# Three more projection jobs ahead of the retention heads, their results kept in DRAM

## The chip, the cores and the metric

One NeuronCore of a Trainium2 chip. The metric is device time in microseconds (us) of one execution. Engines by their short names: PE (TensorE, matmuls), DVE (VectorE), ACT (ScalarE), POOL (GpSimd), SP (SyncE, which issues most loads). A change of about 0.2% is what a measurement of this kernel can tell from none.

## What is computed

One inference step of a two-layer decoder for 512 prompt tokens and 8 x 4 sample tokens (544 columns in all), model width 1024: layer 0 mixes with a short gated convolution, layer 1 with multi-scale retention (4 heads, keys of 256, values of 512), each followed by a SwiGLU block (hidden width 2816). Weights are shared by both groups. The part around the change is the retention mixer:

```python
z = x @ w_in                                  # q, k (1024 each), v, g (2048 each)
q, k, v, g = jnp.split(z, [1024, 2048, 4096], axis=-1)
q = rotary(q, pos); k = rotary(k, pos) * (256 ** -0.5)
# per head, chunks of 128 tokens:
scores = jnp.einsum('bhid,bhjd->bhij', qc, kc) * decay
inner  = jnp.einsum('bhij,bhjv->bhiv', scores, vc)
cross  = jnp.einsum('bhid,bhdv->bhiv', qc, S) * cross_w
S_new  = S * chunk_decay + jnp.einsum('bhjd,bhjv->bhdv', kc * state_w, vc)
# group norm over each head's 512 values, gain, then
out = (silu(g) * of) @ w_out
```

All values are fp32. The sample tokens also update a recurrent state per head that is read and written.

## The kernel before

Activations lie transposed: 8 tiles of 128 rows by 544 columns, handled as two halves of 272. Every fp32 matrix is split into a high part and a low part (`split`: ACT copies the rounded high part, DVE subtracts to get the low one), and a product takes three matmuls (high-high, high-low, low-high). A plain projection of one output tile of 128 (`project`, L167 to L182, matmuls at L175) takes 8 k-tiles x 3 x 2 halves = 48 matmuls of 272 columns. Weights are loaded on SP's queue in pieces of 512 KB into three buffers (`wts`), split, and used.

A **Job** (L461) makes two output tiles at once from seven products of half size in the manner of Strassen and Winograd (`weights7` builds the sums of weights; matmuls at L480): 7 x 4 x 3 = 84 matmuls in place of 96. Its weights come in two loads, L434 (`w3`) and then L435 (`w1`); two accumulating DMAs on POOL's queue make low parts. `summed` gathers the products: ACT takes snapshots (L540), DVE adds (L543). The feed-forward layers run as such jobs.

At the end of the first feed-forward layer `ahead` (L785) runs while the sums of the activations for jobs can still be kept: it projects q and k of head 0 plainly, then runs five jobs: two gate tiles of head 0, and the four gate tiles of heads 1 and 2 each (`AHEAD = (1, 2)`). Their results go to DRAM (`qk_made`, `gate_made`) from ACT's queue and are loaded again in the heads.

Then come the four heads in a loop (L1298). In each: `value` (L987) projects the values into four PSUM banks and, after its second weight piece, splits q and k, makes the sample scores and transposes the keys; then state, scores, outputs (`inner`), sample outputs and state updates; each output row is normalized on DVE with a power on POOL (`normalized`), transposed on PE (L1172) and multiplied into the gate on DVE (`gated`). Work that depends on none of that fills in between, through `fill(n)` (n = 0 to 3) and by calls at the head's end:

- head 0: gate tiles 2 and 3 of its own, k of head 1; at the end q of head 1
- heads 1 and 2: the output projection of the previous head (`held_project`, two tiles of 24 matmuls in each fill, from the old gated tiles that `held_parts` splits); at the end k, then q, of the next head
- head 3: its four gate tiles (`gate_project`) in the fills; then the old output projection, tiles 4, 5, 2, 3 at places where normalizations run, the halves of tiles 0 and 1 that come from the old head, and `last_project` with its own.

`qk_project` multiplies the projection with a table that holds decay and the inverse norm (`gt`, L915, scaled by `qk_scale` at L942) and `rotate` turns it (L969 to L974, six DVE operations). Head 0's q and k come from DRAM (`qk_loaded`, L926 and L930).

The order of instructions on each engine is set by a list scheduler at build time: program order is the priority, an instruction takes its turn when the scheduler's model has its inputs ready, and each engine then runs its list strictly in order. `tc.issue_after(ins)` puts an instruction behind another one of the same engine. A tile with `bufs=1` and one tag is one place: its next use waits until the last reader of the previous one is done. `rot1` and `gt` in the pool `kp` are such places; the old halves of `held_parts` use both.

Of the kernel before, what the change touches and what calls it, by code (L numbers as in the profile page):

```python
# [49 lines left out]
def hybrid_decode_kernel(ctx: ExitStack, tc: tile.TileContext, a: dict, o: dict):  # L50
# [76 lines left out]
    rN = resid.tile([P, 6], F32, tag="rN", name="rN")  # L127


    last_load = [None]  # L130

    def parts2(n, pool=None, tags=("wh", "wl")):
        return [(pool or wts).tile([P, n], F32R, tag=t, name=nm(t)) for t in tags]
# [294 lines left out]
    def weights7(src1, src2, sw, adding=False):  # L428

        n = KP * P  # L430
        w3, w1 = [wts.tile([P, 2 * n], F32, tag="w", name=nm("w")) for _ in range(2)]
        w2 = sw.tile([P, 2 * n], F32, tag="w2", name=nm("w2"))
        w4 = sw.tile([P, n], F32, tag="w4", name=nm("w4"))
        last_load[0] = nc.sync.dma_start(w3, src2)  # L434
        last_load[0] = nc.sync.dma_start(w1, src1)  # L435
        a11, a12, a21, a22 = w1[:, :n], w1[:, n:], w3[:, :n], w3[:, n:]
        s2, s1 = w2[:, :n], w2[:, n:]
        nc.vector.tensor_add(s1, a21, a22)
        nc.vector.tensor_sub(s2, s1, a11)
        nc.vector.tensor_sub(a21, a11, a21)  # L440
        nc.vector.tensor_sub(w4, a12, s2)
        p1 = parts2(2 * n)
        (split_adding if adding else mixed)(*p1, w1, src1)
        p2 = parts2(2 * n, sw, ("h2", "l2"))
        split(*p2, w2)
        p3 = parts2(2 * n)
        mixed(*p3, w3, src2)
        p4 = parts2(n, sw, ("h4", "l4"))
        split(*p4, w4)

        def part(p, at):
# [328 lines left out]

    dram = ctx.enter_context(tc.tile_pool(name="dram", bufs=1, space=bass.MemoryType.DRAM))
    qk_made = [dram.tile([P, 2, T], F32, tag=f"qk{w}", name=nm("qkm")) for w in range(2)]
    gate_made = {h: dram.tile([P, 4, T], F32, tag=f"g{h}", name=nm("gm")) for h in (0, *AHEAD)}

    def ahead(tp, fp, sw, operand_tiles):  # L785


        wide("m")
# [44 lines left out]
        def gates(h, n):  # L833
            made = {}

            def tile2():
                if not made:
                    made[0] = tp.tile([P, 2, T], F32, tag="gu", name=nm("gate"))
                return made[0]

            def gate(what, src):
                g = tile2()
                if what == "c21":
                    nc.scalar.activation(g[:, 1, :HT], src, AF.Copy)
                elif what == "c12":
                    r = R.rearrange("p a b -> p (a b)").unsqueeze(1).to_broadcast([P, 2, T])
                    nc.vector.tensor_mul(g, g, r)
                    nc.scalar.activation(g, g, AF.Silu)
                    for i in range(2):
                        nc.scalar.activation(g[:, i, :], g[:, i, :], AF.Copy, scale=g_ret(h * 4 + n + i))  # L850
                    nc.scalar.dma_start(gate_made[h][:, n : n + 2, :], g)

            return Job([a["rtg"][h, n + i] for i in range(2)], operand, sw, summed(tile2, gate))

        jobs = [gates(0, 0)] + [gates(h, n) for h in AHEAD for n in (0, 2)]
        jobs[0].prepare()
        run(jobs, (2, 5, 6), lambda i: None, iter(()))

# [3 lines left out]
    with ExitStack() as c2:  # L862
# [47 lines left out]
        def qk_start(h):  # L910

            st = {}
            gt = kp.tile([P, 2, T], F32, tag="gt", name=nm("gt"), bufs=1)
            with tc.issue_after(last_load[0].ins) if h == 0 else ExitStack():
                nc.sync.dma_start(gt, a["gtab"][h])  # L915
            st["gt"] = gt
            st["rot"] = [
                pool.tile([P, 2, T], F32, tag=f"rot{w}", name=nm("rot"), bufs=1) for w, pool in enumerate((tp, kp))
            ]
            return st  # L920

        def qk_loaded(st):

            for t, src in ((st["rot"][1], qk_made[1]), (st["rot"][0], qk_made[0])):
                with tc.issue_after(last_load[0].ins):
                    nc.sync.dma_start(t, src)  # L926
            for which in (1, 0):
                qk_scale(st, which)
# [11 lines left out]
        def qk_scale(st, which):  # L940
            gi = halves(st["gt"][:, which, :])
            nc.vector.tensor_mul(gi, gi, R)  # L942

        def qk_project(h, st, which, dt, inside=None):

# [154 lines left out]
            return st["gate"][n // 2][:, n % 2, :] if len(st["gate"]) > 1 else st["gate"][0][:, n, :]  # L1100

        def gate_project(h, st, n):
            st.setdefault("gate", [])
            if h == NH - 1 and n % 2 == 0:

                pool, tag = ((kp, "gt"), (qp, "qkhl1"))[n // 2]
                t = pool.tile([P, 2, T], F32, tag=tag, name=nm("gate"), bufs=1)
                st["gate"].append(t)
            elif not st["gate"]:
                st["gate"].append(swapped(True, [P, 4, T], F32, "gate"))  # L1110
# [101 lines left out]
        def sample_outputs(h, st, i):  # L1212
# [7 lines left out]
            with tc.issue_after(last_product[0].ins):  # L1220
                for g in range(4):
# [2 lines left out]
                        start=False, stop=(i == 3), skip_group_check=True,  # L1224
                    )

        def states_update(h, st, i):


# [10 lines left out]
                    )  # L1240
            for w, pu in enumerate(pus):
                Si = S[:, 2 * w : 2 * w + 2, :]
                nc.vector.scalar_tensor_tensor(Si, Si, _gamma(h) ** 4, pu, op0=ALU.mult, op1=ALU.add)  # L1243
            nc.sync.dma_start(rets_out[r, h, dt], S)

        def gated_parts(st):
# [51 lines left out]
        for h in range(NH):  # L1298
            more = h + 1 < NH

            def fill(n):

                if h in AHEAD:
                    for i in range(2):
                        held_project(h, (0, 4, 2, 6)[n] + i)
                elif h:
                    gate_project(h, st, n)
                elif n < 2:

                    gate_project(h, st, n + 2)  # L1310
                else:
                    qk_project(h + 1, nxt, 1, n - 2)

            value(h, st)
            st["S"] = {}
# [19 lines left out]
            if h in AHEAD:  # L1335
                st["gate"] = [swapped(h == 2, [P, 4, T], F32, "gate")]
                nc.sync.dma_start(st["gate"][0], gate_made[h])
            if not more:
                held_parts(h, older)
            yn0 = normalized(inner(h, st, 0))  # L1340
            sample_outputs(h, st, 1)
            yn1 = normalized(inner(h, st, 1))
# [6 lines left out]
                    qk_scale(nxt, which)  # L1349
            with tc.issue_after(last_product[0].ins):  # L1350
                if more:
                    qk_project(h + 1, nxt, int(h > 0), 0)
                else:
                    held_project(h, 4)
            with tc.issue_after(last_product[0].ins):
# [9 lines left out]
                gated(h, st, yn2, 2)  # L1365

            if more:
                qk_project(h + 1, nxt, int(h > 0), 1, inside)
            else:
                held_project(h, 5, single=True)  # L1370
                inside()
                held_project(h, 2, single=True)
            yn3 = normalized(p3)
            if not more:
                held_project(h, 3)
            gated_pair(h, st, (yns, 4), (yn3, 3))
            if more and h:
                qk_project(h + 1, nxt, 0, 0)
                qk_project(h + 1, nxt, 0, 1)
            if not more:  # L1380
                held_project(h, 0, False, single=True)
                held_project(h, 1, False)
# [119 lines left out]
```

## Time and profile before

| what | value |
|---|---|
| median of 3 runs | 1458.8 us (1458.06 to 1460.22) |
| the profiled execution: time, span | 1461.27 us, 1459.5 us |
| mean granted clock of PE | 0.996 |
| busy: PE, DVE, ACT, POOL | 99%, 68%, 45%, 10% of the span |
| DMA | 201.89 MB, mean 138 GB/s |
| jobs ahead | about 598 to 657 us |
| the four heads | about 653 to 1077 us |

All times within the profile are counted from the start of the span. A line of a timeline has start and length in us, engine, source line, operation, the tiles written and read, and in brackets how long the engine was idle before and what released it. SPq and the like are the queue's issues of DMAs. A line number can be a helper's: L190 and L191 are the two halves of every `split`, L175 every plain projection.

### The profile page before, as it was taken

Reading aid. Unit: us, or ns where it says so; the run is one execution under the profiler, and the core shown is the slowest. Engines: PE = TensorE matmul, PEld = TensorE weight load, DVE = VectorE, ACT = ScalarE, POOL = GpSimd, SP = SyncE. Lnnn points to the kernel's source line nnn. Section 1 sums busy time; section 2 is a strip of 40 time slices with the busy share of each in tenths; the row PEclk is TensorE's granted clock in tenths of the full one; section 3 lists DMA queues with packets and bytes.
Section 4 is the critical chain, followed back from the end, with each engine's and each line's share of the span. In section 5 each row is a group of like instructions: output and inputs, shape, how many; then the busy total and the mean of one; then the engine's idle time right before and its main releaser. Section 6 shows DMA issues by size and latency. Waiting matters only on the chain.

```text
span 1459.5 us, 26302 instructions
## 1 busy us (share of the span) xinstructions
PE 1443.8 (99%) x10860; PEld 1369.0 (94%) x10860; DVE 985.7 (68%) x1536; ACT 664.0 (45%) x971; POOL 147.9 (10%) x184
## 2 busy tenths in 40 slices
PE   9999999999999999999999999999999999999997
PEld 8999999999999999997878888878999999999997
DVE  5644679847748648677575765845699848749554
ACT  5222466626526437664223032134386626537334
POOL 0100011101101003210010000000111101101002
PEclk9999999999999999999999999999999999999998
DMA  6222246636536434767353734724666635546432
GB/s 219 82 88 92 86 114 140 150 116 126 143 106 139 124 80 133 195 167 262 125 191 116 258 106 144 274 92 143 175 138 149 153 108 131 131 109 148 119 81 77
DMA packets 84297, 201.89 MB, mean 138 GB/s; under 512 B 8129, under 2 KB 25409, under 8 KB 83921
## 3 DMA queue, kind: packets, MB, share of 16 engines
q1 hardware_dynamic: 67296, 165.91, 35.9%
q0 software_dynamic: 15008, 29.18, 12.2%
q10 hardware_dynamic: 1872, 5.12, 0.9%
q8 instruction: 85, 1.39, 0.4%
q14 instruction: 36, 0.29, 0.1%
HBM read 175.11 MB, written 25.08 MB: 137 GB/s over the span
## 4 chain that ended last, share of the span: by engine, by line
PE 89%; DVE 5%; DMA 3%; ACT 1%; issue 1%; POOL 0%; SPq 0%; DVEq 0%; ACTq 0%; POOLq 0%
PE sm L480 35%; PE mm L175 33%; PE sm L175 7%; PE sm L999 2%; PE sm L1000 2%; PE sm L1001 2%; PE sm L163 2%; PE sm L164 1%; PE sm L165 1%; PE sm L1222 1%; DMA w<-in_ffgu_dram 1%; DVE wl L191 1%; DMA w<-in_rtg_dram 1%; DVE S L1243 1%; DVE ol L191 1%
## 5 line engine op out<-in xcount | busy, mean ns | idle before, releaser
L190 ACT ACTIVATE wh<-w 128x1024 fp32r<-128x1024 f32 (+4 forms) x126 | 115.8, 923 | 318.8 <-PE mm L175 204.9
L480 PE MATMUL sm<-oh,wh 128*128 128x272 f32 x744 | 215.5, 290 | 0.1
L480 PE MATMUL sm<-ol,wh 128*128 128x272 f32 x744 | 214.3, 288 | 0.7 <-DVE ol L191 0.7
L480 PE MATMUL sm<-oh,wl 128*128 128x272 f32 x744 | 213.9, 287 | 0.0
L175 PE MATMUL mm<-xh,wh 128*128 128x272 f32 x844 | 176.3, 290 | 1.1 <-ACT wh L190 1.0
L175 PE MATMUL mm<-xh,wl 128*128 128x272 f32 x844 | 174.5, 289 | 0.4 <-DMA wl<-in_rtqk_dram 0.4
L175 PE MATMUL mm<-xl,wh 128*128 128x272 f32 x844 | 173.9, 287 | 0.0
L480 PE MATMUL sm<-oh,h 128*128 128x272 f32 x568 | 164.1, 289 | 0.5 <-DVE gate L543 0.4
L480 PE MATMUL sm<-oh,l 128*128 128x272 f32 x568 | 163.5, 288 | 0.0
L480 PE MATMUL sm<-ol,h 128*128 128x272 f32 x568 | 163.5, 288 | 0.0
L273 DVE TENSOR_TENSOR x<-x,mm 128x544 f32<-128x544 f32 x90 | 64.7, 719 | 144.7 <-PE mm L175 144.7
L191 DVE TENSOR_TENSOR wl<-w,wh 128x1024 fp32r<-128x1024 f32 (+4 forms) x126 | 134.2, 1071 | 23.7 <-ACT wh L190 22.3
L480 PEld LDWEIGHTS sm<-oh,wh 128*128 128x128 f32 x744 | 139.8, 188 | 2.1 <-ACT gate L540 0.9
L423 ACT ACTIVATE wh<-w 128x1024 fp32r<-128x1024 f32 x97 | 102.8, 1060 | 83.2 <-PE sm L480 56.1
L480 PEld LDWEIGHTS sm<-ol,wh 128*128 128x128 f32 x744 | 139.8, 188 | 0.9 <-DVE ol L191 0.9
L480 PEld LDWEIGHTS sm<-oh,wl 128*128 128x128 f32 x744 | 140.3, 189 | 0.0
L426 POOL DMA_DIRECT2D wl<-in_ffgu_dram x87 | 75.6, 869 | 635.2 <-ACT wl L425 261.5
L175 PEld LDWEIGHTS mm<-xh,wh 128*128 128x128 f32 x844 | 132.2, 188 | 5.4 <-ACT wh L190 1.4
L175 PEld LDWEIGHTS mm<-xh,wl 128*128 128x128 f32 x844 | 131.6, 188 | 0.9 <-DMA wl<-in_rtqk_dram 0.6
L175 PEld LDWEIGHTS mm<-xl,wh 128*128 128x128 f32 x844 | 132.1, 188 | 0.1
L191 DVE TENSOR_TENSOR l<-w,h 128x1024 fp32r<-128x1024 f32 x98 | 93.4, 955 | 27.0 <-ACT h L190 26.4
L480 PEld LDWEIGHTS sm<-oh,h 128*128 128x128 f32 x568 | 107.2, 189 | 1.0 <-ACT wh L423 0.6
(296 smaller groups left out, 3211.8 us busy)
## 6 DMA issues: line engine op xcount, KB each, us to landing
w<-in_ffgu_dram SPq DMA_DIRECT2D x88, 512.0 KB, 3.9
wl<-in_ffgu_dram POOLq DMA_DIRECT2D x87, 256.0 KB, 4.8
w<-in_ffdn_dram SPq DMA_DIRECT2D x96, 192.0 KB, 2.5
S<-in_rets_dram SPq DMA_DIRECT2D x16, 1024.0 KB, 7.0
out_rets_dram<-S SPq DMA_DIRECT2D x16, 1024.0 KB, 4.8
w<-in_cvin_dram SPq DMA_DIRECT2D x21, 512.0 KB, 3.4
w<-in_rtqk_dram SPq DMA_DIRECT2D x16, 512.0 KB, 3.6
w<-in_rtg_dram SPq DMA_DIRECT2D x16, 512.0 KB, 4.1
```

The source lines that it names most:

```text
L163: nc.tensor.matmul(out, lh, rh, start=start, stop=False, skip_group_check=True)
L164: nc.tensor.matmul(out, lh, rl, start=False, stop=False, skip_group_check=True)
L175: last_product[0] = nc.tensor.matmul(half(pt, hf)[:, :HT], w[:, c], act[k][:, hf * HT : (hf + 1) * HT], start=(first and k == ks[0] and i ...
L190: h = nc.scalar.activation(dh, src, AF.Copy)
L191: last_low[0] = nc.vector.tensor_sub(dl, src, dh.bitcast(F32))
L273: last_residual[0] = nc.vector.tensor_add(xk, xk, p)
L423: nc.scalar.activation(wh, w, AF.Copy)
L426: nc.gpsimd.dma_start(wl[:, n:], src[:, n:], accum_op=ALU.add)
L480: last = nc.tensor.matmul(out, w[:, c], b, start=(first and k == 0 and i == 0), stop=(k == KP - 1 and i == 2), skip_group_check=True,)
L999: nc.tensor.matmul(out, xh[kt][:, ts_], wh[:, cw], start=(kt == 0), stop=False)
L1000: nc.tensor.matmul(out, xh[kt][:, ts_], wl[:, cw], start=False, stop=False)
L1001: last = nc.tensor.matmul(out, xl[kt][:, ts_], wh[:, cw], start=False, stop=(kt == KT - 1))
```

## The change

- `ahead` runs eight jobs: the five of before, and three new ones in the order shown below: k of head 2, k of head 3 and the first two gate tiles of head 3. A k job stores its sums unscaled to `k_made` in DRAM.
- In heads 1 and 2, k of the next head is loaded from `k_made`, multiplied by the table and rotated (`k_loaded`); q takes the two places at the head's end that k had, and the two projections after the last `gated_pair` are gone.
- In head 3 the fills are gate tiles 2 and 3, then `held_parts` with old output tiles 2 and 3, then nothing; tiles 2 and 3 leave the end of the head. Gate tiles 0 and 1 are loaded from DRAM.
- The loads of head 0's table and k are ordered behind the load L434 of the last job's weights and no longer behind L435; q's load stays behind L435.

```diff
+    last_load, second_load = [None], [None]
...
-        last_load[0] = nc.sync.dma_start(w3, src2)
+        second_load[0] = nc.sync.dma_start(w3, src2)
         last_load[0] = nc.sync.dma_start(w1, src1)
...
+    k_made = {h: dram.tile([P, 2, T], F32, tag=f"k{h}", name=nm("km")) for h in range(2, NH)}
+    gate_made = {h: dram.tile([P, 4, T], F32, tag=f"g{h}", name=nm("gm")) for h in range(NH)}
...
+            def k(what, src):
+                g = tile2()
+                if what == "c21":
+                    nc.scalar.activation(g[:, 1, :HT], src, AF.Copy)
+                elif what == "c12":
+                    nc.scalar.dma_start(k_made[h], g)
+
+            if n is None:
+                return Job([a["rtqk"][h, 2 + i] for i in range(2)], operand, sw, summed(tile2, k))
...
-        jobs = [gates(0, 0)] + [gates(h, n) for h in AHEAD for n in (0, 2)]
+        jobs = [gates(*hn) for hn in ((0, 0), (1, 0), (1, 2), (2, None), (2, 0), (2, 2), (3, None), (3, 0))]
...
-            with tc.issue_after(last_load[0].ins) if h == 0 else ExitStack():
+            with tc.issue_after(second_load[0].ins) if h == 0 else ExitStack():
                 nc.sync.dma_start(gt, a["gtab"][h])
...
-                with tc.issue_after(last_load[0].ins):
+                with tc.issue_after((second_load if src is qk_made[1] else last_load)[0].ins):
                     nc.sync.dma_start(t, src)
...
+        def k_loaded(h, st):
+            r = st["rot"][1]
+            nc.sync.dma_start(r, k_made[h])
+            with tc.issue_after(last_update[0].ins):
+                nc.vector.tensor_mul(r, r, st["gt"][:, 1, :].unsqueeze(1).to_broadcast([P, 2, T]))
+            rotate(r, *products())
...
         def gate_project(h, st, n):
-            st.setdefault("gate", [])
-            if h == NH - 1 and n % 2 == 0:
-                pool, tag = ((kp, "gt"), (qp, "qkhl1"))[n // 2]
...
+            if n == 2:
+                last = h == NH - 1
+                t = kp.tile([P, 2, T], F32, tag="gt", name=nm("gate"), bufs=1) if last else swapped(True, [P, 4, T], F32, "gate")
+                st["gate"] = [None, t] if last else [t]
...
-                nc.vector.scalar_tensor_tensor(Si, Si, _gamma(h) ** 4, pu, op0=ALU.mult, op1=ALU.add)
+                last_update[0] = nc.vector.scalar_tensor_tensor(Si, Si, _gamma(h) ** 4, pu, op0=ALU.mult, op1=ALU.add)
...
-                elif h:
-                    gate_project(h, st, n)
                 elif n < 2:
                     gate_project(h, st, n + 2)
-                else:
+                elif more:
                     qk_project(h + 1, nxt, 1, n - 2)
+                elif n == 2:
+                    held_parts(h, older)
+                    held_project(h, 2)
+                    held_project(h, 3)
...
-            if not more:
-                held_parts(h, older)
+            elif not more:
+                st["gate"][0] = qp.tile([P, 2, T], F32, tag="qkhl1", name=nm("gate"), bufs=1)
+                nc.sync.dma_start(st["gate"][0], gate_made[h][:, :2, :])
...
-                    qk_project(h + 1, nxt, int(h > 0), 0)
+                    qk_project(h + 1, nxt, 0, 0)
...
-                qk_project(h + 1, nxt, int(h > 0), 1, inside)
+                qk_project(h + 1, nxt, 0, 1, inside)
+                if h:
+                    k_loaded(h + 1, nxt)
             else:
                 held_project(h, 5, single=True)
                 inside()
-                held_project(h, 2, single=True)
             yn3 = normalized(p3)
-            if not more:
-                held_project(h, 3)
             gated_pair(h, st, (yns, 4), (yn3, 3))
-            if more and h:
-                qk_project(h + 1, nxt, 0, 0)
-                qk_project(h + 1, nxt, 0, 1)
```

More of the change, by code (lines that the diff above doesn't have):

```diff
@@ L127, in hybrid_decode_kernel @@
     rN = resid.tile([P, 6], F32, tag="rN", name="rN")
-    last_load = [None]
+    last_load, second_load = [None], [None]
     def parts2(n, pool=None, tags=("wh", "wl")):
@@ L782, in hybrid_decode_kernel @@
     qk_made = [dram.tile([P, 2, T], F32, tag=f"qk{w}", name=nm("qkm")) for w in range(2)]
-    gate_made = {h: dram.tile([P, 4, T], F32, tag=f"g{h}", name=nm("gm")) for h in (0, *AHEAD)}
+    k_made = {h: dram.tile([P, 2, T], F32, tag=f"k{h}", name=nm("km")) for h in range(2, NH)}
+    gate_made = {h: dram.tile([P, 4, T], F32, tag=f"g{h}", name=nm("gm")) for h in range(NH)}
     def ahead(tp, fp, sw, operand_tiles):
@@ L1102, in gate_project @@
         def gate_project(h, st, n):
-            st.setdefault("gate", [])
-            if h == NH - 1 and n % 2 == 0:
-                pool, tag = ((kp, "gt"), (qp, "qkhl1"))[n // 2]
[L1107 to L1110, printed above, removed]
+            if n == 2:
+                last = h == NH - 1
+                t = kp.tile([P, 2, T], F32, tag="gt", name=nm("gate"), bufs=1) if last else swapped(True, [P, 4, T], F32, "gate")
+                st["gate"] = [None, t] if last else [t]
             wh, wl = load_piece(a["rtg"][h, n], KT * P)
@@ L1225, in sample_outputs @@
                     )
+        last_update = [None]
         def states_update(h, st, i):
```

## The prediction

> **What bounds the kernel now.** I read the page first, then the waits of TensorE (PE) stretch by stretch, the chain, and windows around the places that the change touches.
>
> ```profile
> span 1459.5 us, 26302 instructions
> PE 1443.8 (99%) x10860; PEld 1369.0 (94%) x10860; DVE 985.7 (68%) x1536; ACT 664.0 (45%) x971; POOL 147.9 (10%) x184
> ```
>
> PE is busy 99% of the span. A busy PE need not be full, so I look at the step from one matmul to the next. These are pieces of the chain of work that ended last (start us, us, what):
>
> ```profile
> 76.03 11.95 PE mm L175 x96
> ...
> 218.49 73.80 PE sm L480 x588
> ```
>
> An ordinary projection (L175) steps 11.95/96 = 0.1245 us per matmul, a matmul of a job (L480) 73.80/588 = 0.1255 us, and the second piece is seven jobs in a row with no break. So the kernel is a chain of matmuls and the time is their number times 0.125 us, plus breaks. In the stretch 590 to 660 us, which holds the jobs ahead, the waits of PE are led by this row; from 660 to 1050 us, the four heads, the same view names no wait of PE at all:
>
> ```profile
> PE sm L480 <- DVE gate L543: 2.2, 2, 1.8
> ```
>
> One wait in it is 1.80 us long. SP's, DVE's and PE's timelines show how it comes about, in the last two jobs ahead:
>
> ```profile
> 617.86 0.33 SPq L434 DMA_DIRECT2D w<-in_rtg_dram  x1
> ...
> 625.85 0.33 SPq L435 DMA_DIRECT2D w<-in_rtg_dram  x1
> 626.23 0.43 SPq L915 DMA_DIRECT2D gt<-in_gtab_dram  x1
> 626.70 0.42 SPq L926 DMA_DIRECT2D rot<-qkm  x1
> ```
> ```profile
> 629.65 0.69 DVE L439 TENSOR_TENSOR w<-w,w 128x512 f32<-128x512 f32 x1 [1.18 <-DMA w<-in_rtg_dram]
> ...
> 631.24 1.36 DVE L942 TENSOR_TENSOR gt<-gt,R 128x544 f32<-128x544 f32 x2 [0.29 <-DMA gt<-in_gtab_dram]
> 633.19 1.29 DVE L930 TENSOR_TENSOR rot<-rot,gt 128x1088 f32<-128x1088 f32 x1 [0.59 <-DMA rot<-qkm]
> 634.40 0.43 DVE L543 TENSOR_TENSOR gate<-gate,sm 128x272 f32<-128x272 f32 x1
> ```
> ```profile
> 634.88 0.39 PE L480 MATMUL sm<-xh,h 128*128 128x272 f32 x1 [1.80 <-DVE gate L543]
> ```
>
> DVE runs in order. Head 0's table and k arrive late behind the last weights, DVE stands for them (0.29 and 0.59 us), works 2.65 us on them, and only then adds the sum that frees PE's bank. The windows show that the gap costs more than itself (columns: length, busy time and count of PE, PEld, DVE, ACT, POOL, then granted clock, DMA share, GB/s):
>
> ```profile
> 600.00:620.00 20.00, 20.00 (x159) 19.66 (x158) 12.83 (x19) 12.35 (x20) 3.50 (x4) 1.00 0.67 185
> 608.50:619.00 10.50, 10.50 (x86) 10.50 (x86) 7.36 (x12) 8.38 (x13) 1.75 (x2) 1.00 0.45 129
> ...
> 620.00:632.00 12.00, 11.63 (x90) 11.09 (x89) 8.37 (x13) 8.16 (x13) 1.74 (x2) 1.00 0.77 207
> 634.90:638.50 3.60, 3.60 (x20) 3.60 (x21) 3.35 (x9) 0.63 (x1) 0.87 (x1) 0.66 0.96 181
> 638.50:642.00 3.50, 3.50 (x26) 3.50 (x26) 3.23 (x4) 2.75 (x4) 0.00 (x0) 0.86 0.18 42
> ```
>
> After the gap the granted clock is 0.66 for 3.60 us and 0.86 for 3.50: 0.34 x 3.60 + 0.14 x 3.50 = 1.7 us lost again. The stop costs 1.8 + 1.7 = 3.5 us. The smaller gap in 620 to 632 (12.00 - 11.63 = 0.37 us) left the clock at 1.00.
>
> [...]
>
> **The change, part by part.** *Three jobs for six projections.* Six tiles of 48 matmuls leave the heads (two k tiles each of heads 2 and 3, two gate tiles of head 3): 288 matmuls. Three jobs of 7 products x 12 = 84 come: 252. That is 36 fewer, 36 x 0.125 = **-4.5 us**.
>
> Do three more jobs run without breaks? In 600 to 620 us 159 matmuls take 20.00 us (0.126 each), and a job's length of 10.50 us has 7.36 us of DVE and 8.38 of ACT: both fit, with two POOL accumulations (1.75 us of POOL). A k job has neither silu nor gains, so less ACT. Its store (544 KB, ACT's queue) ends long before its load. The one small break in this row of jobs (0.37 us) may repeat: between 0 and 3 x 0.37 = 1.1, I take **+0.5 us**, the middle.
>
> *Head 0's table and k earlier.* They now go out behind the load of L434 (617.86) and not behind L435 (625.85): 8 us sooner, when the later weights are not in flight. For 544 KB the page of DMA issues gives:
>
> ```profile
> rot<-qkm SPq DMA_DIRECT2D x2, 544.0 KB, 5.4
> ...
> gate<-gm SPq DMA_DIRECT2D x1, 544.0 KB, 13.8
> ```
>
> So they land about 618.7 + 5.4 = 624, ahead of L439, and DVE's 2.65 us of work need not stand before that L543. I take the whole stop away: **-3.5 us**; the other bound is 0, if the work lands in front of another add that PE wants.
>
> *k through DRAM in heads 1 and 2.* The load waits for the tile of the previous head's old halves. The table's tile, freed by the filler before, was loaded at 808.83; the last state update, behind which the new multiplication is ordered, is here:
>
> ```profile
> 808.83 0.33 SPq L915 DMA_DIRECT2D gt<-in_gtab_dram  x1
> ```
> ```profile
> 832.30 2.35 DVE L1243 SCALAR_TENSOR_TENSOR S<-S,mm 128x1024 f32<-128x1024 f32 x2
> ```
>
> The half that k needs is free one filler later (48 matmuls, 6 us), so the load runs from about 815 and is covered even at 13.8 us. Behind it on SP stand the weights of the value stage and the states, both early by tens of us. The last head's first gate half (544 KB) likewise waits for the scores (before 999.74, below) and is wanted past 1024.
>
> *The changeover between heads, two fillers shorter.* In heads 1 and 2 the two q projections at the end (12 us of PE) go; heads 1 and 2 will change over as head 0 already does, with q last and then the values. That changeover today:
>
> ```profile
> 746.28 1.21 DVE L191 TENSOR_TENSOR wl<-w,wh 128x1024 fp32r<-128x1024 f32 x1
> 747.41 0.71 DVE L972 TENSOR_TENSOR rot<-rot,sqacc 128x544 f32<-128x544 f32 x1
> ...
> 749.83 0.81 DVE L1148 TENSOR_SCALAR yn<-sm,mv,rs 128x512 f32<-128x512 f32 x1 [0.44 <-POOL rs L227]
> ...
> 758.08 0.18 DVE L1198 TENSOR_TENSOR ss<-mm,cb 32x32 f32<-32x32 f32 x1 [2.92 <-PE mm L1194]
> ```
> ```profile
> 750.70 0.66 PE L1172 MATMUL mm<-cb,yn 128*128 128x128 f32 x4
> 751.11 0.48 PE L999 MATMUL sm<-wh,xh 128*128 128x512 f32 x1
> ...
> 757.74 0.29 PE L1194 MATMUL mm<-rot,rot 128*32 128x32 f32 x4
> ```
>
> PE does not stop there today, so there is nothing to gain, but DVE is nearly full. New there is k's multiplication (1.29, as L930) and its six rotation steps of 0.71: 5.6 us. The weights' low half is done at 747.49 and wanted at 751.11: 3.6 us of room. If all of k goes before it, it is 2.0 us late; if it goes after, into the 2.92 us that DVE idles later, nothing is lost. Nothing decides between 0 and 2.0, so I take 1.0 for each changeover: **+2.0 us**. (Two weight splits fewer on ACT and DVE come with the removed tiles and are in this picture already, since head 0's changeover lacks them too.)
>
> *The last head.* Fillers 0 and 1 become gate tiles 2 and 3, filler 2 becomes two tiles of the old output projection (24 matmuls each), filler 3 is empty: nothing waits there, since scores, states and weights have the first three as cover. The old halves must now be split before filler 2:
>
> ```profile
> 994.08 0.39 PE L163 MATMUL sm<-vh,knh 128*128 128x512 f32 x1
> ...
> 999.74 0.41 PE L175 MATMUL mm<-xh,wh 128*128 128x272 f32 x2
> ```
> ```profile
> 1010.35 2.90 ACT L190 ACTIVATE xh<-gate 128x544 fp32r<-128x544 f32 x4 [2.22 <-PE mm L175]
> ```
>
> 2.90 us of ACT in the 5.66 us between the last reader of those tiles and the filler: no cost. At the end two of these tiles are missing as cover for the last normalization:
>
> ```profile
> 1034.18 0.74 PE L175 MATMUL sm<-xh,wh 128*128 128x272 f32 x2
> ...
> 1041.82 0.60 PE L1172 MATMUL mm<-cb,yn 128*128 128x128 f32 x4
> ...
> 1047.36 0.41 PE L175 MATMUL sm<-yh,wh 128*128 128x272 f32 x2
> ```
> ```profile
> 1039.21 0.81 DVE L1148 TENSOR_SCALAR yn<-sm,mv,rs 128x512 f32<-128x512 f32 x1
> ...
> 1043.60 2.63 DVE L191 TENSOR_TENSOR yl<-gate,yh 128x544 fp32r<-128x544 f32 x4 [0.40 <-ACT yh L190]
> ```
> ```profile
> 1042.91 2.30 ACT L190 ACTIVATE yh<-gate 128x544 fp32r<-128x544 f32 x4 [0.31 <-DVE gate L1178]
> ```
>
> From 1034.18 PE will have only the two held first halves, 48 x 0.125 = 6.0 us, to 1040.2; the normalized tile is ready at 1040.0 as now, since state updates stand before it. From the transposes (1041.82) to the first finished part of yl (1043.60 + 2.63/4 = 1044.26) is 2.4 us. So PE, free again about 1040.5 after the transposes, waits till 1042.6: 2.1 us. If the transposes fit inside the last held tile, as they do now, 1.2. If the normalization comes sooner (one split and two residual additions fewer on DVE), near 0. I take **+1.5 us**.
>
> **Sum.** -4.5 + 0.5 - 3.5 + 2.0 + 1.5 = -4.0 us. The profiled execution took 1461.27 with its span of 1459.5; the span would be 1455.5. The median of the three runs, 1458.8, is 2.5 below that execution; the same difference on it gives **1454.8 us**.
>
> **Rivals.** *All new waits are absorbed.* The order of the engines' work shifts so that the k rotation and the last normalization hide. For it: no wait of PE from 660 to 1050 in any head today. Against: DVE's load at the changeover. -4.5 - 3.5 = -8.0: 1450.8.
>
> *The moved loads bring nothing.* Their tiles are not free sooner, or DVE stands for them at an earlier place and holds another add. For it: in-order DVE, and L439 itself waited 1.18 us for weights. Then the 3.5 us stay: -0.5, 1458.3.
>
> *DVE becomes the bound at both changeovers (slower).* In the order of the program the k rotation precedes the last normalization and the splits of the value weights. If DVE keeps to that, 5.6 + 0.81 us come before the low half: 6.4 - 3.6 = 2.8 us late, and a gap of over 1.8 us costs 1.7 more by the clock: 4.5 each. -4.5 + 0.5 - 3.5 + 1.5 + 9.0 = +3.0: 1461.8. It decides the sign from 3.0 us per changeover on, where 2 x 3.0 eats the other four terms (6.0). Against it: short additions that wait on a predecessor leave openings, and the split at 746.28 stands in one, ahead of L972.
>
> **How the numbers follow.** What this kernel's measurement can tell from no change is about 0.2%, 2.9 us: faster is below 1455.9, slower above 1461.7. Forecast 0.45 (its own range 1453 to 1457, from the bounds of the last-head and changeover terms), absorbed 0.17, moved loads bring nothing 0.18, DVE the bound 0.20. Faster: 0.17 and 0.38 of the forecast, 0.55. Same: the rest of the forecast and the idle loads, 0.25. Slower: 0.20, all from the third rival. The range runs from the absorbed case to the middle of the slower one, 1450.8 to 1461.8; beyond it lie half of the third rival and half of the first.
>
> **What would show it.** 10824 matmuls in place of 10860. Right: no wait of PE on L543 of 1.8 us, and a granted clock of 1.00 through the jobs; a PE gap of 0 to 2 us at the second weight piece of the values in heads 2 and 3, its releaser DVE's wl; a gap of 1 to 2 us before the first yh matmul. Wrong: the clock below 1.00 anywhere in the heads (third rival), or the stop still among the jobs (second), or breaks longer than 0.4 us in each of the new jobs.

## The result, and the profile after

The changed kernel takes 1463.6 us (median of 7 runs, 1460.8 to 1468.0) against 1458.8 (7 runs, 1458.1 to 1461.1): 4.8 us more, a ratio of 1.0033, 95% interval 1.0022 to 1.0043. The prediction said 1454.8, with 1461.8 as the upper end of its range: the time moved the other way, and lies above the range.

Span and busy time of the page after:

```profile
span 1460.7 us, 26326 instructions
PE 1439.0 (99%) x10824; PEld 1363.6 (93%) x10824; DVE 997.3 (68%) x1559; ACT 675.7 (46%) x994; POOL 153.7 (11%) x190
```

The 36 matmuls are gone (10824). Here are the waits of PE from 590 to 1060 us after (total, times, longest). Before, the same stretch has the row of 2.2 us that the prediction shows, and one of 0.4 us for weights ahead of the jobs:

```profile
PE mm L1189 <- DVE yn L1165: 3.7, 2, 1.8
PE sm L1189 <- DVE yn L1165: 1.7, 2, 0.8
PE sm L480 <- DVE gate L543: 1.6, 3, 0.9
PE sm L480 <- ACT gate L852: 1.4, 1, 1.4
PE sm L1239 <- DMA S<-in_rets_dram: 0.9, 1, 0.9
```

L1189 holds the transposes of the normalized tiles, L480 the matmuls of the jobs, L1239 the outputs of a state. Windows show where the time lies (start and end, length, then busy time and count of PE, PEld, DVE, ACT, POOL, then granted clock, DMA share, GB/s). After:

```profile
596.50:687.10 90.60, 87.65 (x677) 85.21 (x676) 63.19 (x111) 58.83 (x94) 12.66 (x16) 1.00 0.73 191
687.10:846.00 158.90, 158.65 (x989) 127.39 (x988) 102.30 (x154) 48.51 (x65) 6.06 (x6) 1.00 0.50 175
846.00:882.00 36.00, 33.34 (x199) 27.40 (x198) 30.69 (x51) 5.36 (x5) 3.72 (x4) 0.96 0.64 224
882.00:952.00 70.00, 70.00 (x451) 55.90 (x450) 40.84 (x60) 19.77 (x27) 1.97 (x3) 1.00 0.50 175
952.00:978.00 26.00, 23.34 (x138) 18.28 (x136) 22.96 (x40) 3.41 (x4) 2.28 (x2) 1.00 0.48 162
978.00:1048.00 70.00, 69.09 (x457) 56.57 (x456) 46.33 (x76) 24.51 (x36) 3.58 (x6) 1.00 0.54 168
```

and before, the jobs and then the heads:

```profile
597.90:656.90 59.00, 56.83 (x426) 55.13 (x426) 41.97 (x75) 38.31 (x61) 7.36 (x10) 0.97 0.65 173
656.90:1047.40 390.50, 390.24 (x2515) 321.19 (x2514) 254.95 (x391) 111.50 (x150) 17.27 (x21) 1.00 0.51 172
```

Length minus PE's busy time is PE's idle time. Before, 2.17 us in the jobs and 0.26 in all four heads. After, 2.95 in the jobs, then 0.25, 2.66 at the changeover from head 1 to 2, none, 2.66 at the one from 2 to 3, 0.91 in the last head: 9.43 against 2.43, so +7.0, against -4.5 from the matmuls. That makes +2.5. The two profiled spans differ by 1.2 only, since the changed kernel's execution came to its jobs 1.4 us sooner, before anything that the change touches. (Over the profiled executions of all kernels here, the jobs begin between 595.9 and 598.1 us, though no edit touches what stands ahead of them.) The first long piece of the jobs in the chain, before and then after:

```profile
598.02 22.88 PE sm L480 x179
```
```profile
596.64 22.88 PE sm L480 x179
```

The changeover on DVE's timeline after (start, duration, and in brackets what it waited for), and PE's row that waits for it:

```profile
866.33 1.28 DVE L961 TENSOR_TENSOR rot<-rot,gt 128x1088 f32<-128x1088 f32 x1
867.53 0.78 DVE L979 TENSOR_TENSOR rot<-sm,gt 128x272 f32<-128x272 f32 x2
868.23 0.69 DVE L1161 BATCH_NORM_STATS2 bst<-sm 128x6 f32<-128x512 f32 x1
...
874.81 0.71 DVE L993 TENSOR_TENSOR rot<-rot,rt 128x544 f32<-128x544 f32 x1
875.45 0.14 DVE L226 TENSOR_SCALAR rs<-mv 128x1 f32<-128x1 f32 x1
...
877.16 0.81 DVE L1165 TENSOR_SCALAR yn<-sm,mv,rs 128x512 f32<-128x512 f32 x1 [0.44 <-POOL rs L227]
```
```profile
878.03 0.65 PE L1189 MATMUL mm<-cb,yn 128*128 128x128 f32 x4 [1.83 <-DVE yn L1165]
```

The statistics of the last tile are ready at 869.6. Then DVE does the rotation steps of k and q until 875.45, and only then the small step that POOL's power needs; the normalization itself begins at 877.16, 7.5 us after its statistics. PE has its transposes next in its order and stands 1.83 us, with value matmuls still behind them.

### The profile page after: what moved, and what is told of

It reads as the page before. It is cut to its first block, busy times and chain, and to the rows that moved or that the text cites. A ratio compares the mean times of both kernels' runs of the same rounds, so it can differ in the third digit from the quotient of the medians.

```text
span 1460.7 us, 26326 instructions
## 1 busy us (share of the span) xinstructions
PE 1439.0 (99%) x10824; PEld 1363.6 (93%) x10824; DVE 997.3 (68%) x1559; ACT 675.7 (46%) x994; POOL 153.7 (11%) x190
## 4 chain that ended last, share of the span: by engine, by line
PE 86%; DVE 7%; DMA 3%; ACT 2%; issue 1%; POOL 1%; SPq 0%; DVEq 0%; ACTq 0%; POOLq 0%
PE sm L480 36%; PE mm L175 31%; PE sm L175 7%; PE sm L163 2%; PE sm L1020 1%; PE sm L164 1%; PE sm L1021 1%; PE sm L165 1%; PE sm L1019 1%; PE sm L1239 1%; DMA w<-in_ffgu_dram 1%; DMA gt<-in_gtab_dram 1%; DVE S L1262 1%; DVE wl L191 1%; DMA S<-in_rets_dram 1%
## 5 line engine op out<-in xcount | busy, mean ns | idle before, releaser
L480 PE MATMUL sm<-oh,wh 128*128 128x272 f32 x768 | 222.5, 290 | 0.1
L480 PE MATMUL sm<-ol,wh 128*128 128x272 f32 x768 | 221.3, 288 | 0.1
L480 PE MATMUL sm<-oh,wl 128*128 128x272 f32 x768 | 220.7, 287 | 0.0
L480 PE MATMUL sm<-oh,h 128*128 128x272 f32 x592 | 170.9, 289 | 2.1 <-ACT gate L852 1.4
L480 PE MATMUL sm<-ol,h 128*128 128x272 f32 x592 | 169.9, 287 | 0.0
L480 PE MATMUL sm<-oh,l 128*128 128x272 f32 x592 | 169.9, 288 | 0.0
L175 PE MATMUL mm<-xh,wh 128*128 128x272 f32 x756 | 157.4, 289 | 0.3 <-ACT wh L190 0.3
L175 PE MATMUL mm<-xh,wl 128*128 128x272 f32 x756 | 156.6, 289 | 0.1
L175 PE MATMUL mm<-xl,wh 128*128 128x272 f32 x756 | 156.2, 288 | 0.0
L480 PEld LDWEIGHTS sm<-oh,wh 128*128 128x128 f32 x768 | 144.3, 188 | 2.3 <-ACT gate L540 1.1
L480 PEld LDWEIGHTS sm<-oh,wl 128*128 128x128 f32 x768 | 144.8, 189 | 0.0
L480 PEld LDWEIGHTS sm<-ol,wh 128*128 128x128 f32 x768 | 144.3, 188 | 0.4 <-DVE ol L191 0.4
L191 DVE TENSOR_TENSOR wl<-w,wh 128x1024 fp32r<-128x1024 f32 (+4 forms) x120 | 127.1, 1064 | 22.7 <-ACT wh L190 21.3
L175 PEld LDWEIGHTS mm<-xh,wh 128*128 128x128 f32 x756 | 118.3, 188 | 3.6 <-ACT vh L1057 0.8
L175 PEld LDWEIGHTS mm<-xh,wl 128*128 128x128 f32 x756 | 117.9, 188 | 0.9 <-DMA wl<-in_rtqk_dram 0.3
L175 PEld LDWEIGHTS mm<-xl,wh 128*128 128x128 f32 x756 | 118.4, 188 | 0.2 <-DVE xl L205 0.2
L480 PEld LDWEIGHTS sm<-oh,h 128*128 128x128 f32 x592 | 111.5, 188 | 3.1 <-ACT gate L852 1.5
```

Of the source, the lines that this page charges most:

```text
L175: last_product[0] = nc.tensor.matmul(half(pt, hf)[:, :HT], w[:, c], act[k][:, hf * HT : (hf + 1) * HT], start=(first and k == ks[0] and i ...
L191: last_low[0] = nc.vector.tensor_sub(dl, src, dh.bitcast(F32))
L480: last = nc.tensor.matmul(out, w[:, c], b, start=(first and k == 0 and i == 0), stop=(k == KP - 1 and i == 2), skip_group_check=True,)
```

## The experiments

**Theory.** The loss is four separate waits: k's work ahead of the last normalization on DVE; ACT's list in the jobs, and weights without a free buffer; the fourth state of the last head. **Rivals:** the prediction's prices, or engines that are full, so that a wait taken away comes back elsewhere. Times are medians; "before" is the kernel before in runs beside the same kernels, 1457.9 to 1458.8.

### The last normalization ahead of k's work

```diff
                 qk_project(h + 1, nxt, 0, 1, inside)
-                if h:
-                    k_loaded(h + 1, nxt)
...
             gated_pair(h, st, (yns, 4), (yn3, 3))
+            if more and h:
+                k_loaded(h + 1, nxt)
```

> The changed kernel, with the load, multiplication and rotation of k written after the last normalization and its transposes. Theory A (the rotation stands on DVE ahead of the power's input and so of the last normalized tile, and PE's transposes stand for it): the 2.0 us gap at the transposes of heads 1 and 2 goes, together with the half-clock window that it can set off, so 4 to 7 us less than the changed kernel, about 1457 to 1460. Rival (DVE is simply full there, and whatever is put second makes PE wait): a gap of about 2 us comes back at the sample scores or at the second piece of the value weights, and the time stays within 1 us of the changed kernel's 1463.

1461.05 us, ratio to before 1.0013 (1.0005 to 1.0022): 2.6 us less than the changed kernel, where at least 4 were expected. The longest waits of PE in it:

```profile
PE sm L480 <- DVE gate L543: 1.7, 3, 1.0
PE sm L1189 <- DVE yn L1165: 1.7, 2, 0.8
PE sm L1239 <- DMA S<-in_rets_dram: 1.5, 1, 1.5
PE sm L480 <- ACT gate L852: 1.4, 1, 1.4
```

The row `mm L1189`, 3.7 us, is gone, so the order of the program made it. Little of it came back: new waits of 0.3 us each for DVE and for ACT stand at the start of head 2, where the rival expected 2 us. What the run came short by is in part the state's wait, 1.5 where it was 0.9, which in this trace is followed by a stretch of 3.4 us at a granted clock of 0.50; the changed kernel's trace has its one such stretch behind a gap of 1.83 us.

### A filler again behind the first state

```diff
-                elif n == 2:
-                    held_parts(h, older)
-                    held_project(h, 2)
-                    held_project(h, 3)
+                else:
+                    if n == 2:
+                        held_parts(h, older)
+                    held_project(h, n)
```

> The changed kernel, with the two old output tiles of the last head spread over fillers 2 and 3, one each, in place of both in filler 2. Theory B (with filler 3 empty the fourth state, whose load can only start when the first state has been written out, arrives 0.9 us too late for PE): the wait of PE on the state's load goes, 1.2 us less than the changed kernel, about 1462. Rival (the state's load is late by DMA traffic, wherever the filler is): the wait stays and the time is the same.

1464.83 us, ratio 1.0042 (1.0029 to 1.0054). The row of L1239 is gone from the waits, so the empty filler is what laid it bare, but the time did not fall: the first yh matmul stands at 1050.27 us, 2.2 later than in the changed kernel, 0.8 of which it was late already where the jobs began. What the new order costs in its place is settled in part only. The held tile now runs inside a group of eight L1239 matmuls, and the two and the six take 1.02 and 1.04 us by PE's timeline, where a whole group takes 1.04 in the changed kernel: about 1 us. A later run removes the same wait in another way.

### A buffer of its own for the second weights

```diff
-        w3, w1 = [wts.tile([P, 2 * n], F32, tag="w", name=nm("w")) for _ in range(2)]
+        w3 = wts.tile([P, 2 * n], F32, tag="w", name=nm("w"))
+        w1 = (spare or wts).tile([P, 2 * n], F32, tag="f" if spare else "w", name=nm("w"))
...
+        for job in jobs[2:]:
+            job.spare = fp
```

> The changed kernel, with one of the two weight tiles of the third to eighth job ahead placed in the tile of the feed-forward operands, which is free by then, so that five buffers carry weights and not three. Theory C (from the third job on each second weight load starts only when the previous job has split its last weights, lands 4 to 5 us later, and the jobs run 1 to 1.5 us too long): DVE no longer waits 1 to 2.4 us for weights, the four gaps of 0.5 to 1.5 us among the jobs (3.6 us in all) shrink to under 1 us, 2.5 to 4 us less than the changed kernel. Rival (DVE and ACT are too loaded with a gate's own steps beside the splits): the gaps stay above 2.5 us in all although the weights are there early, and the time falls by under 1 us.

1462.31 us, ratio 1.0022 (1.0013 to 1.0032), 1.3 less. The waits at the jobs:

```profile
PE sm L482 <- ACT gate L854: 1.4, 1, 1.4
...
PE sm L482 <- DVE gate L545: 0.7, 2, 0.4
```

The gap of 0.9 us goes, the one of 1.4 stays: two causes, and the buffer was one. PE's idle time in the jobs falls from 2.95 to 2.11 us.

### The gains behind the next job's copies

The two gain activations and the store of a gate job are issued at the sum `c11` of the next job, behind the copies that free PE's bank.

```diff
-                    for i in range(2):
-                        nc.scalar.activation(g[:, i, :], g[:, i, :], AF.Copy, scale=g_ret(h * 4 + n + i))
-                    nc.scalar.dma_start(gate_made[h][:, n : n + 2, :], g)
+                    late.append(lambda: gains(g))
+                    if h == NH - 1:
+                        late.pop()()
...
+                if what == "c11" and late:
+                    late.pop()()
```

> The changed kernel, but the two gain activations of a gate job (2 x 0.69 us of ACT) and its store are issued behind the first product of the next job's middle. Theory (ACT's list holds the copies that free PE's bank): the gaps of 1.36 and 0.3 us among the jobs go or shrink below 0.4 each, 1 to 1.7 us less: about 1462. Rival (weights that land late set the pace of the jobs): the gap stays or comes back elsewhere among the jobs, no change: 1463.6.

1461.05 us, ratio 1.0024 (1.0015 to 1.0033). That is 2.6 less than the changed kernel, 1.7 if each is taken against its own before. ACT's timeline in the changed kernel ahead of the copies L540 that PE waited for:

```profile
635.18 1.12 ACT L850 ACTIVATE gate<-gate 128x1088 f32<-128x1088 f32 x1
636.21 1.04 ACT L423 ACTIVATE wh<-w 128x1024 fp32r<-128x1024 f32 x1
637.15 1.37 ACT L852 ACTIVATE gate<-gate,vec 128x544 f32<-128x544 f32 x2
638.43 0.62 ACT L425 ACTIVATE wl<-wh 128x512 fp32r<-128x512 f32 x1
...
638.95 0.66 ACT L540 ACTIVATE gate<-sm 128x272 f32<-128x272 f32 x2
```

ACT is busy 46% of the span, but here silu, a split, the gains and another split stand one behind the other in front of a 0.3 us copy. With the gains late the gap of 1.36 us is 0.48, so ACT's list made it. But one of 1.08 behind ACT's gains stands later in the jobs, and PE's idle time there is 2.87 us where it was 2.95: by place the rival is right, and the shorter time of this run is not explained by the jobs. Late gains and the buffer together, in the run below that also gives the fourth state a buffer, leave 1.22 us.

### The parts alone on the kernel before

The moved loads:

> The kernel before, with the loads of head 0's table and k moved ahead of the last job's second weight load, and nothing else of the change. Theory D (these loads caused the stop of 1.8 us and its half-clock window): the stop goes and the time is 3.5 us below the kernel before, about 1455.3. Rival (DVE only stands for them at another place, or the weights then land later): the stop is still there, shifted, and the time stays within 1 us of 1458.8.

1457.44 us, ratio 0.9990 (0.9981 to 0.9999): -1.1 us. The stop of 1.80 us is gone, and one gap is left in the jobs. DVE's row and PE's:

```profile
624.34 0.73 DVE L942 TENSOR_TENSOR gt<-gt,R 128x544 f32<-128x544 f32 x1 [1.05 <-DMA gt<-in_gtab_dram]
```
```profile
629.61 0.39 PE L480 MATMUL sm<-oh,h 128*128 128x272 f32 x1 [0.75 <-DVE gate L543]
```

This is the add that held PE for 0.37 us before, at 627.04. DVE now stands for the table and scales it ahead of that add, 1.8 us in all, and the gap has grown to 0.75. PE's idle time in the jobs falls from 2.17 to 0.75: -1.4, not -1.8.

The two k jobs, with what goes with them in heads 1 and 2:

> The kernel before with only the k part of the change: two k jobs, k loaded in heads 1 and 2, two fillers less there; the loads of table and k, the last head and its gates stay as before. Theory (the k part carries the loss): 168 matmuls in place of 192, -24 x 0.125 = -3.0; the gap of 1.36 us among the jobs +1.4; two changeovers with gaps of 0.83 and 1.83 at the transposes, +5.3; half of the 1.83 gaps set off 1.7 us of half clock, +1.7. Sum +5.4: 1464. Rival (the prediction's price for it, 1.0 per changeover and 0.3 among the jobs): -3.0 + 0.3 + 2.0 = -0.7: 1457.9.

1465.0 us, ratio 1.0043 (1.0031 to 1.0056), 7.1 us more than before, where the theory said 5.4 and the prediction's prices -0.7. Its longest waits of PE:

```profile
PE mm L1192 <- DVE yn L1168: 3.7, 2, 1.8
PE sm L1192 <- DVE yn L1168: 1.6, 2, 0.8
PE sm L480 <- DVE gate L543: 1.5, 3, 0.7
PE sm L480 <- ACT gate L852: 1.4, 1, 1.4
```

Both changeovers are here in full, without any of the rest. Matmuls (-3.0), PE's idle time in the jobs (2.91 where it was 2.17) and at the changeovers (+5.3) come to +3.1. The profiled execution has a mean clock of 0.996, as that of the changed kernel with its one stretch at half clock (1.7 us), but two of the five runs, with a mean clock of 0.998, took 1463.9 and 1465.4 us all the same. So some 2 to 4 us of the 7.1 are not explained.

The gate job with the last head's part:

> The kernel before with only the gate part: one more gate job, and the last head's fillers, held tiles and gate load as in the change; k and the loads of head 0 stay as before. Theory: 84 matmuls in place of 96, -1.5; one more job +0.4 to +1.4; the wait for the fourth state in the last head 0.9 to 1.5 and half of the time 1.7 of half clock. Sum about +1: 1459.6, and the trace shows the wait at L1239 (or its line here) on the DMA of S and no gap ahead of the first yh matmul. Rival (the prediction's price): no state wait, 1.5 us ahead of the first yh matmul, 0.2 among the jobs: +0.2, 1458.8. The place of the gap tells them apart, not the time.

1463.27 us, ratio 1.0033 (1.0020 to 1.0045): 5.4 more, where the theory expected about 1 and the prediction's price was 0.2. Its longest waits of PE:

```profile
PE sm L480 <- DVE gate L543: 3.4, 3, 2.6
PE sm L480 <- ACT gate L852: 1.4, 1, 1.4
PE mm L175 <- DMA wl<-in_rtqk_dram: 0.6, 1, 0.6
PE sm L1239 <- DMA S<-in_rets_dram: 0.6, 1, 0.6
```

The place is as the theory had it: the state's wait, and none ahead of the first yh matmul. The size was missed in part because the old stop is longer with a sixth job and without the moved loads: 2.6 us in place of 1.8, followed by a stretch of 3.40 us at a granted clock of 0.50 (from 655.76 us). The losses of the parts (-1.1, +7.1, +5.4) add up to 11.4, far more than the +4.8 of the whole. Waits that overlap explain only about 1 us of that: PE's idle time in the jobs changes by -1.4, +0.7 and +2.5 in the parts, together +1.8, and by +0.8 in the whole. The rest is open.

The changed kernel with the loads back at their old place:

> The changed kernel with head 0's table and k loaded again behind the last weights, as before the change; all else as changed. The prediction's price for the move: 3.5 us, so 1467.1. Theory (the move takes away a stop of 1.8 us, and half a clock window in few runs only; 1.1 us measured on the kernel before): 1464.7. Rival (in the changed kernel late weights hold the jobs anyway and the move is worth nothing): 1463.6. The trace should show again a stop of PE on L543 near the end of the jobs.

1463.86 us, ratio 1.0042 (1.0030 to 1.0055), beside 1463.63 and 1.0033 for the changed kernel: 0.2 us by the medians, 1.3 by the ratios. The intervals alone would still allow the 3.5 of the prediction. The waits do not:

```profile
PE sm L480 <- DVE gate L543: 1.7, 3, 0.7
```

No stop of 1.8 us came back. In the changed kernel this row reads 1.6, 3, 0.9, and PE's idle time in the jobs is 2.95 us there and 3.07 here: the move is worth next to nothing in the changed kernel, as the rival has it.

### All mended

Three of the edits above together (normalization first, buffer for the second weights, gains late), and in the last head the outputs of the fourth state behind the next held tile:

```diff
+            if more:
+                sample_outputs(h, st, 3)
...
                 held_project(h, 5, single=True)
+                sample_outputs(h, st, 3)
+                yns = normalized(st["po"])
```

> Four edits on the changed kernel together: the last normalization ahead of k's work (2.6 us by the earlier run), the w1 weights of jobs 3 to 8 in buffers of their own (1.3), the gains late (1.0), and in the last head the outputs of the fourth state placed behind the next held tile instead of ahead of it (1.3, and its share of half clock). Theory (the gaps are separate and none comes back): 1463.6 - 6.2 = 1457.4 or less. Rival (DVE and ACT are the limit in these stages and the waits come back at other places): 1460 or more.

1458.26 us, ratio 1.0000 (0.9991 to 1.0009). Of the long waits in it one is new:

```profile
PE mm L1204 <- DVE yn L1180: 2.3, 1, 2.3
```

The sample tile is normalized later now, and its transposes wait: here a wait did come back. So the next run puts these outputs back and gives that state another buffer, the old gate tile:

```diff
-            S = st["S"][i] = sp.tile([P, 4, DV], F32, tag="S", name=nm("S"))
+            if h == NH - 1 and i == 3:
+                S = st["S"][i] = swapped(True, [P, 4, T], F32, "S")[:, :, :DV]
+            else:
+                S = st["S"][i] = sp.tile([P, 4, DV], F32, tag="S", name=nm("S"))
```

> The changed kernel with: the last normalization ahead of k's work, w1 of jobs 3 to 8 in buffers of their own, gains late, and the fourth state of the last head loaded into the old gate tile, which is free once the old halves are split, so that it need not wait until the first state is written out. Against the earlier combination (1458.26) the outputs of the fourth state are back at their place, so its gap of 2.32 us at the transposes and its share of half clock should go. Theory (the state's wait comes from its buffer): no gap at the state's matmuls nor at the transposes of the last head, 1458.3 - 2.3 - 0.6 = 1455.4. Rival (DVE is late there anyway): a gap of over 1 us stays in the last head, 1457.5 or more.

1457.0 us, ratio 0.9993 (0.9984 to 1.0002). SP issues the load in the changed kernel, and here:

```profile
1023.47 4.31 SPq L1263 DMA_DIRECT2D out_rets_dram<-S  x2
1027.90 2.17 SPq L1227 DMA_DIRECT2D S<-in_rets_dram  x1
```
```profile
1000.79 0.38 SPq L1245 DMA_DIRECT2D S<-in_rets_dram  x1
```

27 us sooner, because it need not wait until the first state is written out. The view of waits then names no state and no transpose in the last head. The time is 1.6 us above the expectation: the gaps of 0.83 us at the third tile stay, as expected, and a new one of 0.8 us stands at the value weights of head 0.

With the third tile's transposes 12 matmuls later in q's projection:

> As the run beside it, and the transposes of the third normalized tile stand 12 matmuls (1.5 us) later in the projection of q. Theory (the two gaps of 0.82 us are only this: DVE finishes that tile 0.8 us after PE asks): both go and nothing follows: 1455.4 - 1.6 = 1453.8. Rival (the later transposes make the last pair of transposes, and the values behind them, wait as long): the gaps come back there, 1455.4.

1457.43 us, ratio 0.9994 (0.9986 to 1.0003): no gain over the run before it. The two gaps of 0.83 us are gone, and smaller ones stand in their place:

```profile
PE sm L482 <- DVE gate L545: 1.2, 3, 0.5
PE sm L1037 <- DVE gate L1213: 0.7, 2, 0.3
```

Last, the same mending without the k jobs (moved loads, gate job, gains late, both buffers):

> The moved loads and the gate part of the change without the k part (k of heads 2 and 3 projected in the heads, as before), with gains late, w1 in buffers of their own and the fourth state in the old gate tile: 12 matmuls fewer than before. Theory (the k part is worth nothing even with its order mended, since its two jobs bring back in small gaps what their matmuls save): moved loads -1.1, matmuls -1.5, one job's breaks +0.4: 1458.5 - 2.2 = 1456.3, no worse than the kernel with all three jobs mended the same way (1457.0). Rival (the k part pays its 3.0 us once its order is mended): about 2 us slower than that one, 1459.

1457.3 us, ratio 0.9989 (0.9980 to 0.9998). It is the lowest ratio of these kernels, level with the moved loads alone (0.9990), and 1.0 us above the 1456.3 that the theory said. Beside 0.9993 with all three jobs mended, the k part brings nothing that these intervals can tell, even in the best order found.

## Why the prediction was wrong, step by step

**Matmuls, -4.5: right.** 10824, and PE's windows between the waits are full.

**Breaks among the jobs, +0.5: 2.6.** Idle time in the jobs without the old stop went from 2.17 - 1.80 = 0.37 to 2.95. I took the small break seen before (0.37) as what may repeat. The new gaps are of another kind: ACT's list in front of a copy (1.36, which the late gains cut to 0.48, though as much came back later in the jobs) and weights without a free buffer (0.9, gone with the spare one). With both mended 1.22 us of idle time is left in the jobs. The windows that I read, 7.36 us of DVE and 8.38 of ACT in a job of 10.5, say that the work fits, not that it comes in the order in which PE needs it.

**Moved loads, -3.5: -1.1 on the kernel before, little in the changed one.** Two faults. The stop did go, but the loads made DVE stand ahead of an earlier add, and a gap of 0.37 us became 0.75; this is the second rival's mechanism, in small. And the 1.7 us of half clock belong to the profiled execution (1461.27), not to the median (1458.8): of 82 runs of the kernel before beside these experiments, 68 have a mean clock of 0.998, where the profiled one has 0.996. I subtracted it from an execution that had it, and then carried the difference over to a median that mostly had not.

**Changeovers, +2.0: 5.3 of idle time, and 1.7 of half clock at one of them (3.40 us at a granted clock of 0.50, from 878.95 us).** This is the largest miss, and it is the third rival's mechanism. I had bounded the cost by the low half of the value weights (3.6 us of room) and wrote that nothing decided the order. The order of the program did: `k_loaded` stands before the last normalization, and DVE's timeline shows it followed. The rival said so, but put the price at the value weights; PE stood at the transposes, which come before them in its list. The 0.83 us at the third tile were in no case of mine. On DVE's timeline two steps of a state update, 1.2 us each, stand between that tile's statistics and its normalization; no run took them away from there.

**Last head, +1.5 ahead of the first yh matmul: none there, 0.9 elsewhere.** The sentence that failed is "filler 3 is empty: nothing waits there". The fourth state uses the first one's buffer, so its load goes out only when the first is written; SP's row at 1027.90, shown above, is this load, and the filler had hidden it.

**The sum.** -4.5 + 2.6 - 1.8 + 5.3 + 0.9 = +2.5 of PE's time by the profile. The medians differ by 4.8. Half clock is a part of the rest: of the two gaps of 1.83 us in the changed kernel's profiled execution one was followed by 3.40 us at a granted clock of 0.50, which is 1.7 more, and in the run with a buffer for the second weights both were. A run of 1460 us that loses 1.7 us in this way has a mean clock lower by 0.0012, and the 7 runs of the changed kernel have 0.994 to 0.997, where the kernel before mostly has 0.998. That it is all of the rest is not shown: three of these runs have the same 0.997 and took 1460.8, 1463.8 and 1464.2 us, and a run of the changed kernel with its loads back had 0.998 and took 1463.6. What else lengthened them is open. That the order of the engines' work and the buffers carry the loss is shown by mending them: with the normalization first, the gains late and both buffers, the same number of matmuls takes 1457.0 us, and the loss is gone.

## What to carry to other kernels

This kernel, with PE busy 99% of its span, had little slack in its lists. Instructions put on DVE or ACT in place of matmuls cost more than they saved while they stood ahead of the one that PE waited for next, so read the order of the program at that place before the sum of busy times. For every filler that goes, list what it hid, the loads behind a buffer's release included. And before a saving is carried from a profiled execution to a median, ask whether the median has that loss at all.

## What the runs showed of the hardware

The clock did not fall from the gap on. Before, the stop of 1.80 us ended at 634.88 us; the granted clock was 1.00 until 636.03, 0.50 from there to 639.45, then 1.00 again. Windows around one gap of each changeover, in the run with a buffer for the second weights:

```profile
874.08:877.48 3.40, 1.57 (x9) 1.00 (x8) 2.96 (x5) 1.06 (x1) 1.39 (x1) 1.00 0.09 33
877.49:880.89 3.40, 3.40 (x11) 2.73 (x10) 3.40 (x8) 1.11 (x1) 0.00 (x0) 0.50 0.00 0
...
969.66:973.05 3.39, 1.56 (x10) 1.04 (x9) 2.95 (x4) 0.95 (x1) 1.39 (x1) 1.00 0.08 31
973.06:976.46 3.40, 3.40 (x10) 2.63 (x9) 2.07 (x7) 0.00 (x0) 0.00 (x0) 0.50 0.00 0
```

Here 3.4 us in which PE stands for 1.83 are followed by one stretch of 3.40 us at a clock of 0.50, and behind it the clock is 1.00 again (880.90 to 884.30 us and 976.48 to 979.80 us). The two slow stretches begin 95.57 us apart, which is 28 times 3.413. So whether a gap costs 1.7 us more may depend on when it begins in a row of such stretches: an estimate from this distance and from the 3.40 us of each, and not shown beyond these traces. In the changed kernel itself the second gap began at 971.0 us. Counted on from its slow stretch in this way (878.95 + 27 x 3.413 = 971.1), that is 0.1 us ahead of the next beginning, and no slow stretch followed:

```profile
967.60:971.10 3.50, 3.40 (x15) 2.43 (x13) 3.50 (x7) 0.75 (x2) 0.56 (x1) 1.00 0.81 285
971.12:974.50 3.38, 1.67 (x10) 1.45 (x11) 2.94 (x5) 0.30 (x1) 0.81 (x1) 1.00 0.05 19
974.60:977.90 3.30, 3.30 (x23) 1.94 (x21) 1.54 (x6) 0.23 (x1) 0.00 (x0) 1.00 0.00 0
```

In six windows of 3.4 us in the traces of this case, PE stood for 1.49 to 2.60 us in one gap, and 3.40 us at a clock of 0.50 followed each: 1.80 us before, 1.83 in the changed kernel, 1.49 with the normalization first, 1.83 twice with the buffer for the second weights, 2.60 with the gate part alone. The gap of 1.36 us in the changed kernel's jobs was followed by a clock of 1.00 (640.03 to 643.40 us). Why 1.7 us of idle time in one stretch (971.12 to 974.50 us) cost no more when the gap began just ahead of it is open.
